# RWKV recurrence with row-packed operands and 64-row products on one Trainium2 core

## The chip, the cores and the metric

The kernel runs on 1 core of one Trainium2 chip. The metric is the device time of one execution in microseconds. Before the change the median of 3 runs is 1753.23 us (1751.1 to 1754.99).

## What is computed

A decoder trunk of two layers on 512 positions of width 1024, all in float32. Each layer has a token mixer of three branches (RWKV-7 time mixing, chunked retention, a spatial gating unit), gates that merge them, and a gated MLP with a short convolution. The change touches the RWKV-7 branch alone, whose core is a recurrence over positions, for 8 heads with a state of 64 x 64 each:

```python
S_t = S_{t-1} (diag(w_t) - kk_t^T (a_t * kk_t)) + v_t^T k_t
y_t = S_t r_t
```

Here w is a decay per channel, k, v and r are projections of the input, and kk is the normalised key.

## The kernel before, in words

**Layout.** Activations lie transposed: 128 channels on the partitions, 512 positions along the free dimension. A tile of 128 channels holds two heads, head h = 0 on partitions 0 to 63 and h = 1 on 64 to 127. Four such tiles, m = 0 to 3, hold the 8 heads. The list `hv` holds the two partition halves.

**Projections.** All large products are split in three: a float32 operand becomes a high part (a rounded copy made by ScalarE, L134) and a low part (the remainder, made by VectorE, L135), and three matmuls (L151) sum high x low, high x high and low x high. A weight unit is 128 x 512 and feeds 12 matmuls of 128 x 512. Units are loaded by DMA, split a few units ahead, and used in a fixed order.

**The recurrence in chunks.** The 512 positions are cut into 8 chunks of 64. Within a chunk the recurrence becomes products of 64 x 64 matrices and one triangular solve.

`prep(m)` (L459 to L527), once for each m, makes the chunk operands on VectorE, ScalarE and GpSimd:
- decayed copies of r and kk (the tile `ag`, L494 and L496) and of kk * a and k (`bk`, L500 and L504). They are written per head, on 64 partitions at a time, because `ag` keeps the two heads in separate free positions: `ag[hv[h], h]` holds the operands of head h, and `ag[hv[1-h], h]` later holds the products of the same head, so that one 128-row operand carries the state's part and v's part together;
- their products for every chunk (L511, 64 rows to 128 columns), which ScalarE copies from PSUM into `GB` and into `ag` (L514, L515), and GpSimd masks to be causal (L505);
- a scaling of `bk` by the decay ratio `F` between chunks, on GpSimd (L520);
- a row sum by the matrix `bonesR` (L524, L525), and VectorE's product with v (L526).

The calls of `prep` alternate with the projections of the next tile (L532 to L543).

`solve` (L667 to L727) inverts the triangular matrices on VectorE, in blocks of 32, with small matmuls for the off-diagonal block (L714, L723).

The chunk loop (L572 to L646) then runs chunk after chunk. `W[c]` is a tile of 128 rows per head: the state on one half of the partitions and v on the other (`vpair`, L558 to L566, brings v there by a transpose). For each chunk:
1. TensorE transposes `bk` (L582); ScalarE copies the result to `bt` (L586).
2. With 128 rows at once, `ag` times `w` gives the part of y (L592) and of x (L595) that come from the state and v.
3. x is copied to `xb`, half by ScalarE, half by VectorE (L596, L597).
4. 64-row products: `bt` times v into the next state `pn` (L603), and the solved `GB` times `xb` into `pu` (L605).
5. `pu` is copied over the state's half of `w` (L606, L607).
6. 64-row products of that with `bt` into `pn` (L612) and with `GB` into y (L614).
7. VectorE adds the scaled old state `fS` to `pn`, per head (L622), which writes the state half of the next `W`. GpSimd scales it for the chunk after (L626).

**What sets the order.** Between steps 2, 4 and 6 stand fills: `self.fill(n, True)` issues the next pieces of other work, mainly the gate projections (12 matmuls each), so that TensorE has something to do while a result is copied. The matmuls of the chunk loop are kept in program order by `po`; other instructions are put in order by a scheduler when the kernel is built. PSUM holds 4 tiles `sm` for this work and 4 tiles `acc` for the large products. A `fill(35)` stands inside `solve`.

Of the kernel before, what the change touches and what calls it, by code (L numbers as in the profile page):

```python
# [17 lines left out]
S = 512  # L18
# [5 lines left out]
FILL = (35, 2, 1)  # L24
# [23 lines left out]
class Emit:  # L48
# [345 lines left out]
    def rwkv(self, l, nst):  # L394
        nc, V, A, a = self.nc, self.nc.vector, self.nc.scalar, self.a
        T, P = nc.tensor, nc.gpsimd
        q8 = lambda t: t.rearrange("p (c t) -> p c t", t=64)
        pcol = lambda n, w: self.pc[:, PC[n]:PC[n] + w]
        omu = self.small((128, 14), "omu", bufs=1)
        po = self.tc.keep_in_program_order if l == 0 else lambda i: i  # L400
# [7 lines left out]
        nkk = self.small((128, 4), "nkk")  # L408
# [41 lines left out]
        hv = [slice(0, 64), slice(64, 128)]  # L450
        AG, BK, Vf, bv = [], [], [], []
        kc, rc = [], []

        def cols3(m):
# [4 lines left out]
        def prep(m):  # L459
# [8 lines left out]
            ag = self.rw((128, 2, 8, 128), "ag", 4)  # L468
# [16 lines left out]
            Eout = ci  # L485
# [4 lines left out]
            V.reciprocal(f, cx[:, 1:8, 0])  # L490
            V.tensor_tensor(f, f, cx[:, 0:7, 64], op=MUL)
            A.activation(tha, pA, AF.Tanh, scale=0.5, bias=haw[:, m:m + 1])
            for h in range(2):
                V.tensor_tensor(ag[hv[h], h, :, 64:128], q8(r)[hv[h]], Ein[hv[h]], op=MUL)  # L494
            for h in range(2):
                V.scalar_tensor_tensor(ag[hv[h], h, :, 0:64], q8(k)[hv[h]], self.p("kk", m)[hv[h]], Eex[hv[h]], op0=MUL, op1=MUL)  # L496
            V.scalar_tensor_tensor(kkn, tha, 1.0, k, op0=ADD, op1=MUL)
            A.activation(tha, tha, AF.Identity, scale=hka[:, m:m + 1], bias=oka[:, m:m + 1])
            for h in range(2):
                V.scalar_tensor_tensor(bk[hv[h], :, h, :], q8(kkn)[hv[h]], nkk[hv[h], m:m + 1], q8(Eout)[hv[h]], op0=MUL, op1=MUL)  # L500
            kp = k
            V.tensor_tensor(kp, k, tha, op=MUL)
            for h in range(2):
                V.tensor_tensor(bk[hv[h], :, 1 - h, :], q8(kp)[hv[h]], q8(Eout)[hv[h]], op=MUL)  # L504
            causal = lambda t: P.affine_select(t, t, [[0, 8], [1, 2], [1, 64]], ALU.is_ge, 0.0, base=-1, channel_multiplier=-1)  # L505
            for g in range(2):
                pgs = [self.sm((128, 4, 128)) for _ in range(2)]
                for j in range(4):
                    c = 4 * g + j
                    for h in range(2):  # L510
                        T.matmul(pgs[h][:, j, :], bk[hv[h], c, :, :].rearrange("p a t -> p (a t)"), ag[hv[h], h, c, :], start=True, stop=True)  # L511
                for h in range(2):
                    o = 1 - h
                    A.copy(GB[hv[h], 8 * m + 4 * g:8 * m + 4 * g + 4, :], pgs[h][hv[h]])  # L514
# [12 lines left out]
            AG.append(ag); BK.append(bk); bv.append(kp)  # L527

        if l == 0:
            V.memset(self.rst[:, 0:512:64], 0.0)  # L530
# [20 lines left out]
        self.solve(GB, n2)  # L551


        W, yT = [None] * 8, []
        fS = None
        po = self.tc.keep_in_program_order

        def vpair(c):  # L558
            pv = self.sm((128, 4, 128))
            for m in range(4):  # L560
                po(T.transpose(pv[:, m, :], Vf[m][:, c * 64:c * 64 + 128], self.c("ident")))
            wp = self.rw((128, 2, 4, 2, 64), "cs", 3)
            for i in range(2):
                W[c + i] = wp[:, i]
                for h in range(2):
                    A.copy(W[c + i][hv[1 - h], :, h, :], pv[hv[i], :, 64 * h:64 * h + 64])  # L566

        self.fill(1, True)
        vpair(0)
        for h in range(2):  # L570
            P.memset(W[0][hv[h], :, h, :], 0.0)
        for c in range(8):  # L572
            if c % 2 == 0:
                y = self.r(n="y")
            self.fill(FILL[2], True)
            if c % 2 and c < 7:
                vpair(c + 1)
            w = W[c]
            if c < 7:
                pb = self.sm((128, 4, 128))  # L580
                for m in range(4):
                    po(T.transpose(pb[:, m, :], BK[m][:, c, :, :].rearrange("p a t -> p (a t)"), self.c("ident")))  # L582
                if c % 2 == 0:
                    bts = self.rw((128, 2, 4, 128), "cs", 3)
                bt = bts[:, c % 2]
                A.copy(bt, pb)  # L586

            pxy = self.sm((128, 2, 4, 64))
            px, py = pxy[:, 0], pxy[:, 1]
            for m in range(4):  # L590
                for h in range(2):
                    po(T.matmul(py[hv[1 - h], m, :], AG[m][:, h, c, 64:128], w[:, m, h, :], start=m == 0, stop=False, skip_group_check=True))  # L592
            for m in range(4):
                for h in range(2):
                    po(T.matmul(px[hv[h], m, :], AG[m][:, h, c, 0:64], w[:, m, h, :], start=False, stop=True, skip_group_check=True))  # L595
            A.copy(xb[hv[0]], px[hv[0]])  # L596
            V.tensor_copy(xb[hv[1]], px[hv[1]])  # L597
            self.fill(FILL[2] + (c == 0), True)
            pu, pn = self.sm((128, 4, 64)), self.sm((128, 4, 64))
            for m in range(4):  # L600
                if c < 7:
                    for h in range(2):
                        po(T.matmul(pn[hv[h], m, :], bt[hv[1 - h], m, hv[h]], w[hv[1 - h], m, h, :], start=m == 0, stop=False, skip_group_check=True))  # L603
                for h in (1, 0):
                    po(T.matmul(pu[hv[h], m, :], GB[hv[h], 8 * m + c, 0:64], xb[hv[h], m, :], start=m == 0, stop=True, skip_group_check=True))  # L605
            A.copy(w[hv[0], :, 0, :], pu[hv[0]])  # L606
            V.tensor_copy(w[hv[1], :, 1, :], pu[hv[1]])  # L607
            self.fill(FILL[2], True)
            for m in range(4):
                if c < 7:  # L610
                    for h in range(2):
                        po(T.matmul(pn[hv[h], m, :], bt[hv[h], m, hv[h]], w[hv[h], m, h, :], start=False, stop=True, skip_group_check=True))  # L612
                for h in (1, 0):
                    po(T.matmul(py[hv[1 - h], m, :], GB[hv[h], 8 * m + c, 64:128], w[hv[h], m, h, :], start=False, stop=True, skip_group_check=True))  # L614
            if c < 7:
                wn = W[c + 1]
                for h in range(2):
                    d = wn[hv[h], :, h, :]
                    if c == 0:
                        V.tensor_copy(d, pn[hv[h]])  # L620
                    else:
                        V.tensor_tensor(d, pn[hv[h]], fS[hv[h]], op=ADD)  # L622
# [44 lines left out]
    def solve(self, G, n2):  # L667
# [18 lines left out]
        TS = self.rw((128, 32, 32), "cs", 3)  # L686
        TMP = self.rwp.tile([128, 288], F32, name=self.nm("TMP"))
# [506 lines left out]
```

## Time and profile before

| | |
|---|---|
| median of 3 runs | 1753.23 us (1751.1 to 1754.99) |
| the profiled execution | 1751.58 us |
| its span, first to last instruction | 1749.8 us |
| mean granted TensorE clock | 0.998 |
| TensorE busy in the span | 99% |
| VectorE, ScalarE, GpSimd busy | 66%, 45%, 11% |

The profile is of one execution. A group row gives the line, the engine, the operation, the tiles (out, then in), the shape and the count; then the busy time in us and the mean duration in ns; then the idle time of the engine just before these instructions, with what ended it. A timeline row gives the start in us from the start of the span, the duration in us, the engine and the instruction, with a count where equal neighbours are merged; a bracket gives the idle time before it. PE is TensorE, DVE VectorE, ACT ScalarE, POOL GpSimd. A float32 matmul of the small products appears as two records.

### The profile page before, as it was taken

What the parts mean: (1) busy time and instruction counts of PE and PEld (TensorE: products, weight loads), DVE (VectorE), ACT (ScalarE), POOL (GpSimd) and SP (SyncE); (2) the same over time, 40 slices, a digit from 0 to 9 for tenths busy, and PEclk for the clock granted to TensorE, in tenths of its full rate; (3) what the DMA queues carried; (4) which work ended last, traced back from release to release, by engine and by line L of the source; (5) the groups of instructions that cost most, each with busy time, mean ns of one, the idle gap of its engine ahead of it and who ended that gap; (6) DMA issues with size and microseconds to landing.
All of it is one profiled execution on the core that took longest, in us unless ns stands there. A gap on an engine that the chain in (4) does not pass through costs nothing.

```text
span 1749.8 us, 26360 instructions
## 1 busy us (share of the span) xinstructions
PE 1730.2 (99%) x9910; PEld 1428.4 (82%) x9910; DVE 1161.9 (66%) x1968; ACT 787.1 (45%) x1343; POOL 184.0 (11%) x195
## 2 busy tenths in 40 slices
PE   9999999999999999999999999999999999999997
PEld 7877877888888888888888788778888888888887
DVE  6888845568658777753368876455685687777433
ACT  6564444534345444333355544445343454443322
POOL 1132011003200000000013110110132000000000
PEclk9999999999999999999999999999999999999999
DMA  5224432424442332243331343234254422222332
GB/s 177 85 91 136 136 101 94 132 68 163 163 139 98 99 97 98 67 121 117 109 114 61 98 144 127 92 99 137 67 181 144 138 98 97 97 97 67 103 99 82
DMA packets 104542, 193.83 MB, mean 111 GB/s; under 512 B 12128, under 2 KB 16480, under 8 KB 104416
## 3 DMA queue, kind: packets, MB, share of 16 engines
q1 hardware_dynamic: 89568, 159.69, 28.2%
q10 hardware_dynamic: 10368, 17.78, 3.1%
q0 software_dynamic: 4480, 14.68, 2.6%
q8 instruction: 78, 1.28, 0.3%
q14 instruction: 48, 0.39, 0.1%
HBM read 175.33 MB, written 16.78 MB: 110 GB/s over the span
## 4 chain that ended last, share of the span: by engine, by line
PE 88%; DVE 5%; issue 3%; ACT 2%; DMA 1%; POOL 0%; ACTq 0%; POOLq 0%; DVEq 0%
PE acc L151 82%; PE sm L811 1%; DVE wl L135 1%; DVE ag L496 1%; DVE bk L500 1%; PE sm L592 1%; ACT ag L515 0%; DVE cs L482 0%; ACT GB L514 0%; PE sm L916 0%; PE sm L595 0%; PE sm L612 0%; PE sm L603 0%; PE sm L511 0%; DVE ag L494 0%
## 5 line engine op out<-in xcount | busy, mean ns | idle before, releaser
L151 PE MATMUL acc<-lo,sh 128*128 128x512 f32 x1108 | 432.9, 391 | 0.0
L151 PE MATMUL acc<-hi,sh 128*128 128x512 f32 x1108 | 432.0, 390 | 0.0
L151 PE MATMUL acc<-hi,sl 128*128 128x512 f32 x1108 | 430.9, 390 | 0.0
L134 ACT CAST sh<-wr 128x512 fp32r<-128x512 f32 (+1 forms) x389 | 235.9, 611 | 388.9 <-PE acc L151 300.6
L135 DVE TENSOR_TENSOR sl<-wr,sh 128x512 fp32r<-128x512 f32 (+1 forms) x389 | 262.6, 679 | 185.5 <-PE acc L151 88.8
L151 PEld LDWEIGHTS acc<-lo,sh 128*128 128x128 f32 x1108 | 208.1, 188 | 43.9 <-issue 0.7
L151 PEld LDWEIGHTS acc<-hi,sl 128*128 128x128 f32 x1108 | 208.1, 188 | 43.2
L151 PEld LDWEIGHTS acc<-hi,sh 128*128 128x128 f32 x1108 | 208.1, 188 | 42.7
L151 PE MATMUL acc<-hi,wl 128*128 128x512 f32 x588 | 229.7, 392 | 6.4 <-DVE wl L135 6.4
L151 PE MATMUL acc<-lo,wh 128*128 128x512 f32 x588 | 233.0, 396 | 1.3 <-DVE lo L210 1.3
L151 PE MATMUL acc<-hi,wh 128*128 128x512 f32 x588 | 229.5, 390 | 0.0
L151 PE MATMUL acc<-ah,sh 128*128 128x512 f32 (+1 forms) x748 | 219.4, 377 | 0.0
L135 DVE TENSOR_TENSOR wl<-wr,wh 128x512 fp32r<-128x512 f32 x195 | 142.0, 729 | 115.9 <-ACT wh L134 114.9
L134 ACT CAST wh<-wr 128x512 fp32r<-128x512 f32 x195 | 120.2, 618 | 202.6 <-PE acc L151 172.9
L151 PEld LDWEIGHTS acc<-ah,sh 128*128 128x128 f32 x748 | 137.7, 188 | 25.6
L151 PE MATMUL acc<-ah,sl 128*128 128x512 f32 (+1 forms) x374 | 140.9, 377 | 0.0
L151 PEld LDWEIGHTS acc<-hi,wl 128*128 128x128 f32 x588 | 110.4, 188 | 31.5 <-DVE wl L135 8.4
L151 PEld LDWEIGHTS acc<-lo,wh 128*128 128x128 f32 x588 | 110.4, 188 | 25.5 <-ACT wh L134 1.5
L151 PEld LDWEIGHTS acc<-hi,wh 128*128 128x128 f32 x588 | 110.5, 188 | 21.9
L967 DVE TENSOR_TENSOR fu<-acc,rsF 128x512 f32<-128x512 f32 x88 | 60.8, 690 | 69.5 <-PE acc L151 69.4
L969 ACT ACTIVATE cv<-fu,pc 128x512 f32<-128x512 f32 x88 | 71.9, 817 | 44.0 <-DVE fu L967 39.4
L151 PEld LDWEIGHTS acc<-ah,sl 128*128 128x128 f32 x374 | 70.4, 188 | 12.9
(289 smaller groups left out, 2150.7 us busy)
## 6 DMA issues: line engine op xcount, KB each, us to landing
wr<-wall SPq DMA_DIRECT2D x488, 256.0 KB, 2.6
wr<-wdn SPq DMA_DIRECT2D x80, 256.0 KB, 2.6
gd<-gth ACTq DMA_DIRECT2D x48, 256.0 KB, 3.2
gth<-gd POOLq DMA_DIRECT2D x48, 256.0 KB, 3.4
tab<-rot ACTq DMA_DIRECT2D x8, 256.0 KB, 3.6
xi<-xT SPq DMA_DIRECT2D x8, 256.0 KB, 3.4
wr<-wdn SPq DMA_DIRECT2D x16, 128.0 KB, 2.1
xd<-xi POOLq DMA_DIRECT2D x8, 256.0 KB, 2.6
```

The source lines that it names most:

```text
L134: self.kept(self.nc.scalar.copy(hi[:, :n], raw[:, :n]))
L135: self.kept(self.nc.vector.tensor_tensor(lo[:, :n], raw[:, :n], hi[:, :n], op=SUB))
L151: i = self.nc.tensor.matmul(*x, **y)
L496: V.scalar_tensor_tensor(ag[hv[h], h, :, 0:64], q8(k)[hv[h]], self.p("kk", m)[hv[h]], Eex[hv[h]], op0=MUL, op1=MUL)
L500: V.scalar_tensor_tensor(bk[hv[h], :, h, :], q8(kkn)[hv[h]], nkk[hv[h], m:m + 1], q8(Eout)[hv[h]], op0=MUL, op1=MUL)
L592: po(T.matmul(py[hv[1 - h], m, :], AG[m][:, h, c, 64:128], w[:, m, h, :], start=m == 0, stop=False, skip_group_check=True))
L811: po(T.matmul(X[h][:, i, :], lhsT, rhs, start=new[h], stop=stop, skip_group_check=True))
L967: V.tensor_tensor(u, ps, self.rsF, op=MUL)
L969: A.activation(t, u, AF.Identity, scale=self.p("cw2", j), bias=self.p("cb", j))
```

## The change

The operands of both heads are packed by rows: tile `X` holds r's and kk's decayed copies, head 0 on partitions 0 to 63 and head 1 on 64 to 127, so that each is written by one operation on 128 partitions; tile `Y` holds the products with k, in the same way, with the heads' halves exchanged. `bk` is written in two operations in place of four.

With the state `St` and v (`Vt`) in separate tiles, each 128-row product of the chunk loop becomes two 64-row products: `X` with the state (in the stretch at the start of the chunk), and `Y` with v (moved into the stretch with `bt` and `xb`; for x, a chunk ahead, into the next chunk's tile `Q`). The products in `prep` are cut in two as well, by columns.

The decay ratio `F` no longer scales `bk` on GpSimd. VectorE adds the update to the state and multiplies the sum by `F`, on 128 partitions. The copies to `xb` and `U` are one operation each (VectorE, ScalarE); `bt` is copied in three pieces. The mask on `GB` covers its right half alone; `solve` zeroes one block of it by memset.

```diff
-        xb = self.rwp.tile([128, 4, 64], F32, name=self.nm("XB"))
+        xb, U, St = [self.rwp.tile([128, 4, 64], F32, name=self.nm(n)) for n in ("XB", "U", "S")]
...
-            for h in range(2):
-                V.tensor_tensor(ag[hv[h], h, :, 64:128], q8(r)[hv[h]], Ein[hv[h]], op=MUL)
-            for h in range(2):
-                V.scalar_tensor_tensor(ag[hv[h], h, :, 0:64], q8(k)[hv[h]], self.p("kk", m)[hv[h]], Eex[hv[h]], op0=MUL, op1=MUL)
+            V.tensor_tensor(x[:, :, 64:128], q8(r), Ein, op=MUL)
+            V.scalar_tensor_tensor(x[:, :, 0:64], q8(k), self.p("kk", m), Eex, op0=MUL, op1=MUL)
...
-            for h in range(2):
-                V.scalar_tensor_tensor(bk[hv[h], :, h, :], q8(kkn)[hv[h]], nkk[hv[h], m:m + 1], q8(Eout)[hv[h]], op0=MUL, op1=MUL)
+            V.scalar_tensor_tensor(bk[:, :, 0, :], q8(kkn), nkk[:, m:m + 1], q8(Eout), op0=MUL, op1=MUL)
...
-            for h in range(2):
-                V.tensor_tensor(bk[hv[h], :, 1 - h, :], q8(kp)[hv[h]], q8(Eout)[hv[h]], op=MUL)
+            V.tensor_tensor(bk[:, :, 1, :], q8(kp), q8(Eout), op=MUL)
...
-                    for h in range(2):
-                        T.matmul(pgs[h][:, j, :], bk[hv[h], c, :, :].rearrange("p a t -> p (a t)"), ag[hv[h], h, c, :], start=True, stop=True)
-                for h in range(2):
-                    o = 1 - h
-                    A.copy(GB[hv[h], 8 * m + 4 * g:8 * m + 4 * g + 4, :], pgs[h][hv[h]])
-                    A.copy(ag[hv[o], h, 4 * g:4 * g + 4, :], pgs[h][hv[o]])
+                    for h in range(2):
+                        i = T.matmul(pK[hv[1 - h], j, :], bk[hv[h], c, 1, :], x[hv[h], c, :], start=True, stop=True)
+                        if c or h:
+                            po(i)
+                        po(T.matmul(pB[hv[h], j, :], bk[hv[h], c, 0, :], x[hv[h], c, :], start=True, stop=True))
+                A.copy(GB[:, 8 * m + 4 * g:8 * m + 4 * g + 4, :], pB)
+                A.copy(y[:, 4 * g:4 * g + 4, :], pK)
             for h in range(2):
-                causal(GB[hv[h], 8 * m:8 * m + 8, :].rearrange("p c (a t) -> p c a t", a=2))
-                causal(ag[hv[1 - h], h].rearrange("p c (a t) -> p c a t", a=2))
-            d = bk[:, 0:7].rearrange("p c a t -> p c (a t)")
-            P.tensor_tensor(d, d, f.unsqueeze(2).to_broadcast([128, 7, 128]), op=MUL)
+                yr, gr = y[hv[h]].rearrange("p c (a t) -> p c a t", a=2), GB[hv[h], 8 * m:8 * m + 8, 64:128]
+                P.affine_select(yr, yr, [[0, 8], [1, 2], [1, 64]], ALU.is_ge, 0.0, base=-1, channel_multiplier=-1)
+                P.affine_select(gr, gr, [[0, 8], [1, 64]], ALU.is_ge, 0.0, base=0, channel_multiplier=-1)
...
+        self.fill(FILL[2], True)
+        Q = self.sm((128, 2, 4, 64))
+        for m, h in mh:
+            mm(Q[hv[h], 1, m, :], Y[m][hv[1 - h], 0, 0:64], Vt[0][hv[1 - h], m, :], m == 0)
         for c in range(8):
...
-            for m in range(4):
-                for h in range(2):
-                    po(T.matmul(py[hv[1 - h], m, :], AG[m][:, h, c, 64:128], w[:, m, h, :], start=m == 0, stop=False, skip_group_check=True))
-            for m in range(4):
-                for h in range(2):
-                    po(T.matmul(px[hv[h], m, :], AG[m][:, h, c, 0:64], w[:, m, h, :], start=False, stop=True, skip_group_check=True))
-            A.copy(xb[hv[0]], px[hv[0]])
-            V.tensor_copy(xb[hv[1]], px[hv[1]])
-            self.fill(FILL[2] + (c == 0), True)
+            if c % 2 == 0 and c < 6:
+                vpair(c + 2)
+            for m, h in mh if c else ():
+                mm(P1[hv[1 - h], 0, m, :], X[m][hv[h], c, 64:128], St[hv[h], m, :], m == 0)
+                mm(Q[hv[h], 1, m, :], X[m][hv[h], c, 0:64], St[hv[h], m, :])
+            V.tensor_copy(xb, Q[:, 1])
+            if c < 7:
+                A.copy(bt[:, :, 0:64], pb[:, :, 0:64])
+                for h in range(2):
+                    A.copy(bt[hv[h], :, 64:128], pb[hv[1 - h], :, 64:128])
+            self.fill(FILL[2], True)
+            Q = self.sm((128, 2, 4, 64)) if c < 7 else None
+            for i in (0, 4, 5, 6, 7, 1, 2, 3):
+                for h in range(2):
+                    m, o = i % 4, 1 - h
+                    if c < 7 and i < 4:
+                        mm(Q[hv[h], 0, m, :], bt[hv[o], m, hv[h]], Vt[c][hv[o], m, :], m == 0)
+                    elif c < 7:
+                        mm(Q[hv[h], 1, m, :], Y[m][hv[o], c + 1, 0:64], Vt[c + 1][hv[o], m, :])
+                    if i < 4:
+                        mm(P1[hv[h], 1, m, :], GB[hv[h], 8 * m + c, 0:64], xb[hv[h], m, :], c == m == 0)
+                    else:
+                        mm(P1[hv[o], 0, m, :], Y[m][hv[o], c, 64:128], Vt[c][hv[o], m, :])
+            A.copy(U, P1[:, 1])
+            self.fill(FILL[2], True)
+            for m, h in mh:
+                mm(P1[hv[1 - h], 0, m, :], GB[hv[h], 8 * m + c, 64:128], U[hv[h], m, :])
                 if c < 7:
+                    mm(Q[hv[h], 0, m, :], bt[hv[h], m, hv[h]], U[hv[h], m, :])
             if c < 7:
-                wn = W[c + 1]
-                for h in range(2):
-                    d = wn[hv[h], :, h, :]
-                    if c == 0:
-                        V.tensor_copy(d, pn[hv[h]])
-                    else:
-                        V.tensor_tensor(d, pn[hv[h]], fS[hv[h]], op=ADD)
-                if c < 6:
-                    fS = self.rw((128, 4, 64), "fS", 2)
-                    for h in range(2):
-                        P.tensor_tensor(fS[hv[h]], wn[hv[h], :, h, :], F[hv[h], :, c + 1:c + 2].to_broadcast([64, 4, 64]), op=MUL)
+                f = F[:, :, c:c + 1].to_broadcast([128, 4, 64])
+                if c == 0:
+                    V.tensor_tensor(St, Q[:, 0], f, op=MUL)
+                else:
+                    V.tensor_tensor(St, St, Q[:, 0], op=ADD)
+                    V.tensor_tensor(St, St, f, op=MUL)
...
+        for h in range(2):
+            self.nc.gpsimd.memset(G[64 * h + 32:64 * h + 64, :, 0:32], 0.0)
```

More of the change, by code (lines that the diff above doesn't have):

```diff
@@ L467, in prep @@
                 T.matmul(o, w[:, ms], xh, start=False, stop=True)
-            ag = self.rw((128, 2, 8, 128), "ag", 4)
+            x, y = [self.rw((128, 8, 128), n, 4) for n in ("X", "Y")]
             bk = self.rw((128, 8, 2, 64), "bk", 4)
@@ L526, in prep @@
             V.tensor_tensor(kp, v, pbn, op=MUL)
-            AG.append(ag); BK.append(bk); bv.append(kp)
+            X.append(x); Y.append(y); BK.append(bk); bv.append(kp)
         if l == 0:
@@ L551, in rwkv, with mm @@
         self.solve(GB, n2)
-        W, yT = [None] * 8, []
-        fS = None
-        po = self.tc.keep_in_program_order
+        Vt, yT, mh = [None] * 8, [], [(m, h) for m in range(4) for h in range(2)]
+        def mm(o, l, r, start=False):
+            po(T.matmul(o, l, r, start=start, stop=True, skip_group_check=True))
         def vpair(c):
@@ L574, in rwkv @@
                 y = self.r(n="y")
[L575 to L578, printed above, removed]
+            if c:
+                self.fill(FILL[2], True)
+            P1 = self.sm((128, 2, 4, 64))
             if c < 7:
@@ L594, in rwkv @@
                 for h in range(2):
-                    po(T.matmul(px[hv[h], m, :], AG[m][:, h, c, 0:64], w[:, m, h, :], start=False, stop=True, skip_group_check=True))
-            A.copy(xb[hv[0]], px[hv[0]])
-            V.tensor_copy(xb[hv[1]], px[hv[1]])
-            self.fill(FILL[2] + (c == 0), True)
-            pu, pn = self.sm((128, 4, 64)), self.sm((128, 4, 64))
-            for m in range(4):
-                if c < 7:
-                    for h in range(2):
-                        po(T.matmul(pn[hv[h], m, :], bt[hv[1 - h], m, hv[h]], w[hv[1 - h], m, h, :], start=m == 0, stop=False, skip_group_check=True))
-                for h in (1, 0):
-                    po(T.matmul(pu[hv[h], m, :], GB[hv[h], 8 * m + c, 0:64], xb[hv[h], m, :], start=m == 0, stop=True, skip_group_check=True))
@@ L606, in rwkv @@
[L606 to L610, printed above, removed]
-                    for h in range(2):
-                        po(T.matmul(pn[hv[h], m, :], bt[hv[h], m, hv[h]], w[hv[h], m, h, :], start=False, stop=True, skip_group_check=True))
-                for h in (1, 0):
-                    po(T.matmul(py[hv[1 - h], m, :], GB[hv[h], 8 * m + c, 64:128], w[hv[h], m, h, :], start=False, stop=True, skip_group_check=True))
@@ new lines, in rwkv @@
+            A.copy(U, P1[:, 1])
+            self.fill(FILL[2], True)
+            for m, h in mh:
+                mm(P1[hv[1 - h], 0, m, :], GB[hv[h], 8 * m + c, 64:128], U[hv[h], m, :])
+                if c < 7:
+                    mm(Q[hv[h], 0, m, :], bt[hv[h], m, hv[h]], U[hv[h], m, :])
+            if c < 7:
+                f = F[:, :, c:c + 1].to_broadcast([128, 4, 64])
[4 more added lines that the diff above has]
+                    V.tensor_tensor(St, St, f, op=MUL)
@@ L627, in rwkv @@
+            py = P1[:, 0]
             yr = hv[c % 2]
```

17 lines of the change are left out of this document (6 added, 11 removed).

## The prediction

> **What bounds the kernel now.** I read the page first: engine shares, then the chain that ended last by engine.
>
> ```profile
> span 1749.8 us, 26360 instructions
> PE 1730.2 (99%) x9910; PEld 1428.4 (82%) x9910; DVE 1161.9 (66%) x1968; ACT 787.1 (45%) x1343; POOL 184.0 (11%) x195
> ...
> PE 88%; DVE 5%; issue 3%; ACT 2%; DMA 1%; POOL 0%; ACTq 0%; POOLq 0%; DVEq 0%
> ```
>
> TensorE is busy all the way; VectorE, the next, has a third of the span free. So the question is what the change does to the stream of matmuls, and to the few places where that stream stops. The waits of PE name them, and PE's own timeline shows the four of the first group (each pair: the last matmul before the stop and the first after it).
>
> ```profile
> PE acc L151 <- DVE wl L135: 6.4, 4, 2.7
> ```
>
> ```profile
> 106.62 0.39 PE L151 MATMUL acc<-lo,wh 128*128 128x512 f32 x1
> 106.84 0.39 PE L151 MATMUL acc<-hi,wh 128*128 128x512 f32 x1
> 108.58 0.50 PE L151 MATMUL acc<-hi,wl 128*128 128x512 f32 x1 [1.35 <-DVE wl L135]
> ...
> 132.50 0.39 PE L151 MATMUL acc<-hi,wh 128*128 128x512 f32 x1
> 134.89 0.50 PE L151 MATMUL acc<-hi,wl 128*128 128x512 f32 x1 [2.00 <-DVE wl L135]
> ...
> 969.21 0.39 PE L151 MATMUL acc<-hi,wh 128*128 128x512 f32 x1
> 970.02 0.51 PE L151 MATMUL acc<-hi,wl 128*128 128x512 f32 x1 [0.42 <-DVE wl L135]
> ...
> 993.06 0.39 PE L151 MATMUL acc<-hi,wh 128*128 128x512 f32 x1
> 996.11 0.50 PE L151 MATMUL acc<-hi,wl 128*128 128x512 f32 x1 [2.66 <-DVE wl L135]
> ```
>
> Matmuls follow each other every 0.22 to 0.23 us (first two rows). Start to start the four stops take 1.74, 2.39, 0.81 and 3.05 us; less 0.23 each, the stream loses 1.51 + 2.16 + 0.58 + 2.82 = **7.07 us**. (The brackets give less, because a matmul's modelled end lies behind the next start.) All four are in `prep`, two per layer, and all wait for the low half of a weight, which VectorE splits off at L135 between `prep`'s own operations.
>
> **The change part by part.**
>
> *VectorE in prep.* Here is its queue ahead of the second stop, and the late split of the other three.
>
> ```profile
> 127.16 0.68 DVE L135 TENSOR_TENSOR wl<-wr,wh 128x512 fp32r<-128x512 f32 x1
> ...
> 129.49 1.51 DVE L500 SCALAR_TENSOR_TENSOR bk<-cs,nkk,cs 64x512 f32<-64x512 f32 x2
> ...
> 131.15 1.33 DVE L494 TENSOR_TENSOR ag<-rwc,cs 64x512 f32<-64x512 f32 x2
> 132.50 1.51 DVE L496 SCALAR_TENSOR_TENSOR ag<-rwc,pc,cs 64x512 f32<-64x512 f32 x2
> ...
> 134.18 0.65 DVE L135 TENSOR_TENSOR wl<-wr,wh 128x512 fp32r<-128x512 f32 x1
> ```
>
> ```profile
> 107.84 0.69 DVE L135 TENSOR_TENSOR wl<-wr,wh 128x512 fp32r<-128x512 f32 x1
> ...
> 969.27 0.69 DVE L135 TENSOR_TENSOR wl<-wr,wh 128x512 fp32r<-128x512 f32 x1
> ...
> 995.36 0.69 DVE L135 TENSOR_TENSOR wl<-wr,wh 128x512 fp32r<-128x512 f32 x1
> ```
>
> Each split ends just before its matmul starts. Between two splits stand six half operations, 64 partitions each. The change makes them three of 128 partitions. Does a full one cost what a half one does?
>
> ```profile
> L496 DVE SCALAR_TENSOR_TENSOR ag<-rwc,pc,cs 64x512 f32<-64x512 f32 x16 | 12.0, 748 | 0.2
> L500 DVE SCALAR_TENSOR_TENSOR bk<-cs,nkk,cs 64x512 f32<-64x512 f32 x16 | 12.0, 747 | 1.6 <-ACT cs L486 1.3
> L504 DVE TENSOR_TENSOR bk<-rwc,cs 64x512 f32<-64x512 f32 x16 | 11.0, 686 | 0.4
> L494 DVE TENSOR_TENSOR ag<-rwc,cs 64x512 f32<-64x512 f32 x16 | 10.6, 663 | 0.1
> L502 DVE TENSOR_TENSOR rwc<-rwc,cs 128x512 f32<-128x512 f32 x8 | 5.5, 686 | 0.0
> ```
>
> It does: L504 on 64 partitions and L502 on 128 both take 686 ns. So half of 12.0 + 12.0 + 11.0 + 10.6 = 45.6 us goes: 22.8 us of VectorE, 2.85 us per `prep`. That isn't itself time of the kernel; it counts only where the stream waits. Ahead of a late split, one each of L500, L494 and L496 goes: 0.75 + 0.66 + 0.75 = 2.16 us. The four stops are 1.51, 2.16, 0.58 and 2.82 us, so with nothing else moved min(2.16, stop) goes from each: 1.51 + 2.16 + 0.58 + 2.16 = 6.41 us. The remaining 0.66 us should go too: earlier `prep`s free VectorE in the same way (so the queue ahead of the fourth stop begins earlier), and in the changed kernel's listed order fewer operations stand between two splits there. I take all 7.07 us; bounds: 0 (the queue order puts a split late elsewhere) and 7.07.
>
> *The order.* I compared the listed order of both kernels' instructions, engine by engine. TensorE meets `prep`'s four blocks of products 13, 23, 37 and 66 matmuls earlier than now in the first layer (9 to 50 in the second), and the product with `bonesR` 3 matmuls behind each block instead of 12 to 16. These waits are new in place.
>
> ```profile
> 53.49 1.51 DVE L500 SCALAR_TENSOR_TENSOR bk<-cs,nkk,cs 64x512 f32<-64x512 f32 x2 [0.17 <-ACT cs L486]
> ```
>
> ```profile
> 65.30 2.06 PE L511 MATMUL sm<-ag,bk 64*128 64x128 f32 x32
> 67.29 0.50 PE L151 MATMUL acc<-hi,wh 128*128 128x512 f32 x1
> ```
>
> ```profile
> L514 ACT COPY GB<-sm 64x512 f32<-64x512 f32 x32 | 18.4, 575 | 1.9 <-PE sm L511 1.5 <-ACT gth L377 0.4
> L482 DVE TENSOR_TENSOR_SCAN cs<-rst,cs 128x512 f32<-128x512 f32 x8 | 12.7, 1593 | 3.9 <-ACT cs L481 3.8
> ```
>
> I walked VectorE's listed order with the durations above. Ahead of the first block, from 53.5 us on, stand two scalar_tensor_tensors, three tensor_tensors, three splits and two short ones before `bk` is complete, about 2 × 0.75 + 6 × 0.68 + 0.4 = 6.0 us, so 59.5 us. The block stands 13 matmuls ahead of its place at 65.30, at 65.3 − 13 × 0.227 = 62.3 us: 2.8 us to spare. The tightest place that I found is in the second layer's last `prep`: from the arrival of the decay's product, two steps of ScalarE (about 1.5 us), the scan (1.6) and twelve listed operations up to a split (about 7.5) make 10.6 us, and TensorE has 53 matmuls or their equal, 12.0 us, before it needs that split: 1.4 us to spare. If one slips, the stream waits by the slip. The product with `bonesR` reuses a PSUM tile that ScalarE has to empty with the second of two copies (0.58 us each) after half the block; those end about when the product is due, so up to 0.3 us each could be lost: 0 to 2.4 us over eight; I take 0.
>
> *ScalarE and GpSimd in prep.* Four full copies replace eight halves; the scaling by F leaves GpSimd, one of its two masks per head is half as long, two memsets per layer come. Neither engine is waited for by PE in `prep` now; what needs them first is `solve`, and its first product stands behind fill(35), 35 × 12 × 0.227 = 95 us of matmuls. I cost them at 0; without that cover it would be a few of their operations, 0.6 to 1.6 us each as above.
>
> *TensorE.* The total of its own work is the big unknown. An fp32 product leaves two records (L592: 8 products, x16).
>
> ```profile
> 263.16 0.22 PE L612 MATMUL sm<-cs,cs 64*64 64x64 f32 x2
> 263.17 0.23 PE L614 MATMUL sm<-cs,GB 64*64 64x64 f32 x2
> ...
> 263.45 0.23 PE L612 MATMUL sm<-cs,cs 64*64 64x64 f32 x2
> ...
> 267.06 0.69 PE L592 MATMUL sm<-cs,ag 128*64 128x64 f32 x16
> 267.58 0.64 PE L595 MATMUL sm<-cs,ag 128*64 128x64 f32 x16
> ```
>
> L612 and L614 are 64-row products into all four quadrants (two row halves, two column halves). Four records start within 0.01 us, and the row at 263.45 begins the fifth round after 263.16: 0.058 us a round, so four products (two rounds) take 0.117 us. The 128-row products of L592 take 0.52 us for eight: two column halves run at a time. Now count a chunk c = 1 to 6. Before: 16 products of 128 rows, 2 × 0.52 = 1.04 us, plus 16 + 16 of 64 rows, 8 × 0.117 = 0.94. After: 16 + 32 + 16 products of 64 rows, all ordered so that four in a row meet four quadrants: 16 × 0.117 = 1.87 us. So 1.98 against 1.87. Chunks 0 and 7 come out alike: products that use two quadrants only are as many before as after. The number of stretches between fills stays, and so do the changes of array shape. In `prep`, 16 products of 64×128 become 32 of 64×64, four at a time instead of two: the 1.99 us of the block (65.30 to 67.29) stay. Bounds: −0.11 × 14 chunks = −1.5 us, and, if only two quadrants ever ran together, +1.87 × 14 + 1.99 × 8 = +42 us. I take 0, nearest to the rows at 263.
>
> *Hand-overs in the recurrence.* The state's scaling moves from GpSimd (off the path) to VectorE (on it).
>
> ```profile
> L566 ACT COPY cs<-sm 64x256 f32<-64x256 f32 x32 | 11.7, 366 | 0.6
> L622 DVE TENSOR_TENSOR cs<-sm,fS 64x256 f32<-64x256 f32 x24 | 10.1, 421 | 0.7
> L597 DVE COPY XB<-sm 64x256 f32<-64x256 f32 x16 | 6.8, 427 | 13.3 <-ACT XB L596 13.1
> ```
>
> Before, two half adds (0.84 us) make the next state; after, one full add and one full multiply, about the same. The cover is the fill, 12 matmuls × 0.227 = 2.7 us, and each hand-over (`xb`, `U`, the state) is one or two operations of about 0.4 us behind at most one 0.7 us filler operation: 1.6 us. The tightest place is ScalarE in chunks 0, 2 and 4: four copies of `vpair` and three of `bt`, 7 × 0.37 = 2.6 us against some 2.7 to 3.5. If it slips, what waits is the stretch with `xb`; 0 to 0.5 us each, six times: 0 to 3 us. I take 0.
>
> **Sum.** The profiled execution took 1751.58 us (span 1749.8): 1751.6 − 7.1 = 1744.5. It lies 1.65 us below the median of its three runs, 1753.23; against that median the forecast is **1746 us**.
>
> **Rivals.**
>
> *The stops move.* Splits or products late in new places eat the gain: the `bonesR` product (2.4), `vpair` in chunks 0, 2, 4 (3), one of the four stops left (0.6 to 2.8). Speaks for it: the block of products now stands earlier. Against: every place that I walked has slack. Half of it eaten gives 1750, all of it 1753.
>
> *Quadrants don't run four at a time* (the slower side). Place: all 64-row products. Price: 42 us if two at a time, 1753 − 7 + 42 = 1788. It decides from 7.07 / 42 = 17% of the overlap lost. For it: the new stretches are up to 32 products long, and neighbours in them share rows. Against: in L612 and L614 neighbours share rows too (h = 1 of both), and those four start together. [...]
>
> *More than the stops goes.* If the 1.5 us of the recurrence comes too: 1744.
>
> *The change does nothing:* if the splits are late for their casts or DMAs instead of VectorE, 1753; the rows above show the VectorE queue full up to each split, so little.
>
> **How the numbers follow.** Stops go, stream unchanged (1743 to 1749): 0.75. Stops move and eat most: 0.14, around 1751. Quadrants lose overlap, in part or whole: 0.08, from 1755 up. More goes: 0.03. The range 1742 to 1752 holds the first and the fourth and most of the second. About 0.2%, 3.5 us, is what a measurement of this kernel can tell from no change: faster 0.79, same 0.12, slower 0.09.
>
> **What would show it.** Right: PE's waits for L135 in `prep` vanish, VectorE's sum falls by about 20 us, stretches of 64-row products keep 0.058 us a round, and the time falls by no more than about 8 us. Wrong: a new row of PE waiting for ScalarE or VectorE in the recurrence or at the `bonesR` product; rounds of 0.117 us; or `prep`'s block of 2 us growing to 4.

## The result and the profile after

The changed kernel takes **1743.79 us** (median of 6 runs, 1743.3 to 1746.81) against 1755.28 us for the kernel before (6 runs beside it, 1751.1 to 1757.29). The ratio is 0.9941, with a 95% interval of 0.9928 to 0.9955: 7.9 to 12.6 us less, 10.4 in the middle. The profiled execution took 1744.99 us. These lines of its page are the span, the busy times, and the shares of the chain that ended last.

```profile
span 1743.3 us, 27599 instructions
...
PE 1729.9 (99%) x10614; PEld 1427.2 (82%) x10614; DVE 1116.4 (64%) x1918; ACT 776.2 (45%) x1323; POOL 147.4 (8%) x163
...
PE 94%; issue 2%; DVE 1%; DMA 1%; ACT 1%; POOL 0%; POOLq 0%; SPq 0%; DVEq 0%; ACTq 0%
```

TensorE's busy time is what it was (1730.2 before); the chain's share on VectorE fell from 5% to 1%, and VectorE's busy time fell by 45.5 us, twice what the packed operations save. The waits of PE (us in total, times, longest):

```profile
PE acc L274 <- DVE rst L271: 1.5, 1, 1.5
PE acc L151 <- DVE lo L210: 1.1, 1, 1.1
PE sm L519 <- ACT Y L511: 1.0, 1, 1.0
```

No wait for L135's low half is left. One is new: L519, the product by `bonesR`, waits once for ScalarE. Start to start, from PE's own timeline:

```profile
946.39 0.40 PE L151 MATMUL acc<-hi,wh 128*128 128x512 f32 x1
947.80 0.50 PE L519 MATMUL sm<-lo,bonesR 128*128 128x512 f32 x1 [1.01 <-ACT Y L511]
```

The stream loses 1.41 − 0.23 = 1.18 us there. So the profile shows 7.07 us of stops gone and 1.18 come, a net 5.9 us; the spans differ by 6.5.

Two more differences stand in the two traces. The kernel before loses time once more, inside a block of `prep`'s products (L511), where the list of waits doesn't show it. From its first product to the matmul behind it this block takes 2.95 us, the seven others 1.99; its products start singly, not in pairs, up to 950.5 us, and the second half operation of L504, whose result they need, ends at 950.18 us (that they wait for it is inferred from these times):

```profile
949.32 3.03 PE L511 MATMUL sm<-ag,bk 64*128 64x128 f32 x32
952.27 0.50 PE L151 MATMUL acc<-hi,sh 128*128 128x512 f32 x1
```

```profile
949.49 0.69 DVE L504 TENSOR_TENSOR bk<-rwc,cs 64x512 f32<-64x512 f32 x1
```

In the changed kernel each of the eight blocks takes 1.91 us: 1.6 us less in sum. Against that, the profile after has a slower start: from 7.8 to 10.8 us TensorE runs 9 matmuls in place of 13, and its 40th record starts 1.6 us later. So without the start the spans differ by 8.1 us, of which 5.9 + 1.6 = 7.5 are accounted for. The ratio says 10.4. The rest had to be found.

VectorE's groups in `prep` (mean ns of one in the second figure behind the bar):

```profile
L497 DVE SCALAR_TENSOR_TENSOR bk<-cs,nkk,cs 128x512 f32<-128x512 f32 x8 | 6.0, 748 | 1.8 <-ACT cs L486 1.8
L494 DVE SCALAR_TENSOR_TENSOR X<-rwc,pc,cs 128x512 f32<-128x512 f32 x8 | 6.0, 746 | 0.0
...
L500 DVE TENSOR_TENSOR bk<-rwc,cs 128x512 f32<-128x512 f32 x8 | 5.5, 687 | 0.1
...
L493 DVE TENSOR_TENSOR X<-rwc,cs 128x512 f32<-128x512 f32 x8 | 5.2, 645 | 0.0
```

A full operation costs what a half one did: 22.7 us in place of 45.6. And two groups that nobody touched became shorter; first before, then after:

```profile
L429 DVE SCALAR_TENSOR_TENSOR rwc<-rwp,pc,rwc 128x511 f32<-128x511 f32 x28 | 26.5, 957 | 5.6 <-ACT rwc L428 5.5
```

```profile
L429 DVE SCALAR_TENSOR_TENSOR rwc<-rwp,pc,rwc 128x511 f32<-128x511 f32 x28 | 22.0, 796 | 4.6 <-ACT rwc L428 4.3
...
L482 DVE TENSOR_TENSOR_SCAN cs<-rst,cs 128x512 f32<-128x512 f32 x8 | 10.3, 1285 | 1.4 <-ACT cs L481 1.3
```

L429 fell by 4.5 us, the scan L482 by 2.4 (1593 ns each before). The traces tie this to what GpSimd does beside them: before, 13 of the 28 L429 run beside a GpSimd instruction and take 1203 ns on average, the other 15 take 743; after, it is 4 at 1090 ns and 24 at 747.

### The profile page after: what moved, and what is told of

Its sections match the earlier page's. It is cut to its first block, busy times and chain, and to the rows that moved or that the text cites. A ratio compares the mean times of both kernels' runs of the same rounds, so it can differ in the third digit from the quotient of the medians.

```text
span 1743.3 us, 27599 instructions
## 1 busy us (share of the span) xinstructions
PE 1729.9 (99%) x10614; PEld 1427.2 (82%) x10614; DVE 1116.4 (64%) x1918; ACT 776.2 (45%) x1323; POOL 147.4 (8%) x163
## 4 chain that ended last, share of the span: by engine, by line
PE 94%; issue 2%; DVE 1%; DMA 1%; ACT 1%; POOL 0%; POOLq 0%; SPq 0%; DVEq 0%; ACTq 0%
PE acc L151 87%; PE sm L554 2%; PE sm L808 1%; PE sm L506 1%; DMA wr<-wall 0%; PE sm L913 0%; PE sm L581 0%; PE sm L151 0%; PE sm L478 0%; PE acc L274 0%; DMA ws<-sgw 0%; DMA tab<-rot 0%; PE sm L836 0%; PE sm L863 0%; PE sm L787 0%
## 5 line engine op out<-in xcount | busy, mean ns | idle before, releaser
L135 DVE TENSOR_TENSOR sl<-wr,sh 128x512 fp32r<-128x512 f32 (+1 forms) x389 | 261.9, 677 | 191.3 <-PE acc L151 90.0
L135 DVE TENSOR_TENSOR wl<-wr,wh 128x512 fp32r<-128x512 f32 x195 | 139.7, 718 | 141.0 <-ACT wh L134 139.6
```

What stands on the lines that cost most here:

```text
L135: self.kept(self.nc.vector.tensor_tensor(lo[:, :n], raw[:, :n], hi[:, :n], op=SUB))
```

## The experiments

The theory: VectorE's queue in `prep` makes TensorE's stops, and the packing shortens that queue. The rivals: the gain lies in the recurrence, in GpSimd's lighter load, or in something that the profile of one execution doesn't show. Each ratio is against the kernel before, run beside it.

**VectorE's load alone put back.** In the changed kernel:

```diff
-            V.tensor_tensor(x[:, :, 64:128], q8(r), Ein, op=MUL)
+            for s in hv:
+                V.tensor_tensor(x[s, :, 64:128], q8(r)[s], Ein[s], op=MUL)
...
-            V.tensor_tensor(bk[:, :, 1, :], q8(kp), q8(Eout), op=MUL)
+            for s in hv:
+                V.tensor_tensor(bk[s, :, 1, :], q8(kp)[s], q8(Eout)[s], op=MUL)
```

> The changed kernel with the four packed VectorE operations of prep (X's two, bk's two) each cut into two of 64 partitions, so that VectorE gets back 16 x (0.75 + 0.75 + 0.69 + 0.66) / 2 = 22.8 us and nothing else changes. Theory (VectorE's queue ahead of the weight splits made the stops): stops waiting for L135's low half come back in prep, up to the 7.07 us of before, fewer if what GpSimd left counts too; 1747 to 1751. Rival (the gain comes from the recurrence, from GpSimd or from the end of the layers): no such stop, 1744, within 1.5 us of the changed kernel.

Measured: 1752.27 us (12 runs, 1751.28 to 1754.99), ratio 0.9983 (0.9975 to 0.9992). So 1752.27 − 1743.79 = 8.5 us are gone again with these eight half operations for each `prep` (7.4 by the ratios), a little more than the theory had said. The place is another. PE's waits in this kernel:

```profile
PE sm L523 <- ACT Y L515: 4.9, 3, 2.1
...
PE acc L151 <- DVE wl L135: 1.1, 2, 0.8
```

Most of the stops came back at the `bonesR` product (here L523), not at the splits. The largest of them, by PE's and then ScalarE's timeline:

```profile
88.16 0.40 PE L151 MATMUL acc<-lo,wh 128*128 128x512 f32 x1
90.64 0.50 PE L523 MATMUL sm<-lo,bonesR 128*128 128x512 f32 x1 [2.09 <-ACT Y L515]
```

```profile
88.20 0.72 ACT L428 ACTIVATE rwc<-rwp,omu 128x512 f32<-128x512 f32 x1 [0.84 <-DVE rwp L426]
89.40 0.72 ACT L428 ACTIVATE rwc<-rwp,omu 128x512 f32<-128x512 f32 x1 [0.48 <-DVE rwp L426]
90.03 0.57 ACT L515 COPY Y<-sm 128x512 f32<-128x512 f32 x1
90.49 0.59 ACT L514 COPY GB<-sm 128x512 f32<-128x512 f32 x1
```

Read it from below. The product needs a PSUM tile that the copies empty; the copies stand in ScalarE's queue behind two L428 of the next projections; these wait for VectorE (L426). A late VectorE thus reaches TensorE by way of ScalarE too. In the changed kernel the one stop that is left (at 947.80) has the same two L428 ahead of it:

```profile
945.94 1.34 ACT L428 ACTIVATE rwc<-rwp,omu 128x512 f32<-128x512 f32 x2 [0.84 <-DVE rwp L426]
947.18 0.56 ACT L511 COPY Y<-sm 128x512 f32<-128x512 f32 x1
```

**GpSimd's load alone put back.** In the changed kernel, `ones1` being a tile of ones:

```diff
+            d = bk[:, 0:7].rearrange("p c a t -> p c (a t)")
+            P.tensor_tensor(d, d, self.ones1.unsqueeze(2).to_broadcast([128, 7, 128]), op=MUL)
```

> The changed kernel with the multiply of bk put back on GpSimd, by a tile of ones (the decay stays on VectorE, so the values stay as they are): 8 x 1.8 = 14.4 us of GpSimd come back. Theory (no instruction of TensorE waits for GpSimd in prep): 1744, within 1.5 us. Rival (GpSimd's work lengthens VectorE's beside it: L429 took 957 ns in before and 796 ns in the changed kernel, the scan L482 1593 and 1285, and their sums fell by 6.9 us): part of the gain goes, 1746 to 1748, and L429's or L482's mean rises.

Measured: 1744.97 us (6 runs), ratio 0.9943 (0.9929 to 0.9957); L429 took 804 ns. No loss that can be told: the multiply on GpSimd is not what the gain is made of.

**Both together.** The two diffs above in one kernel.

> Both edits together: VectorE's four operations of prep in halves, and the multiply of bk on GpSimd by ones. Prep's load is then nearly that of before, and the recurrence is that of the changed kernel. Theory (all of the gain lies in prep's load on VectorE): 1750 to 1755, four stops of about 7 us in sum. Rival (a part of the gain lies in the recurrence): stops as before and yet 3 us or more below the kernel before.

Measured: 1754.54 us (12 runs), ratio 0.9995 (0.9986 to 1.0003): all of the gain is gone, though the recurrence is the new one. The recurrence is therefore neutral, within about 2.5 us; in the traces its stretches of small products, each from the first product to the matmul behind it, sum to 48.2 us in the second profile of before (shown below) and to 48.3 in the changed kernel. Against the first experiment, whose 12 runs were taken beside these, the median is 2.3 us higher: 9 of the 12 runs here lie above 1753.4 us, and 2 of the 12 there. So once VectorE is full GpSimd's multiply costs some 2 us, and the trace shows a way: L429 takes 975 ns on average in place of 851, and the stops at the `bonesR` product, which stand where they stood there, are longer (6.3 us in place of 4.9):

```profile
PE sm L527 <- ACT Y L517: 6.3, 3, 3.2
```

**The kernel before, weights split earlier.**

```diff
-AHEAD = {None: 2, "p": 4, "r": 3, "f": 3, "u": 5}
+AHEAD = {None: 2, "p": 6, "r": 3, "f": 3, "u": 5}
```

> The kernel before, with the weight units of prep split up to 6 ahead in place of 4, nothing packed. Theory (a split is late because it stands behind prep's operations in VectorE's queue, and the stop is all that it costs): most of the four stops go without any packing, so 1748 to 1750, 5 to 7 us below the kernel before. Rival (VectorE hasn't the time in prep at all, or buffers come free no sooner): the stops stay or move, within 2 us of the kernel before.

Measured: 1756.1 us (12 runs), ratio 1.0003 (0.9994 to 1.0011), and PE's wait as it was:

```profile
PE acc L151 <- DVE wl L135: 6.8, 4, 3.0
```

The rival holds. A setting that lets the splits go further ahead gives VectorE no time to do so. Whether it is the time or the buffers that bind wasn't told apart.

**VectorE relieved in the kernel before, by GpSimd.**

```diff
-                V.tensor_tensor(ag[hv[h], h, :, 64:128], q8(r)[hv[h]], Ein[hv[h]], op=MUL)
+                P.tensor_tensor(ag[hv[h], h, :, 64:128], q8(r)[hv[h]], Ein[hv[h]], op=MUL)
```

> The kernel before with r's decayed copy (L494, two operations of 0.66 us for each prep) on GpSimd in place of VectorE, nothing packed: 10.6 us leave VectorE. Theory (VectorE's queue makes the stops): about 1.33 us of each stop go, 1.33 + 1.33 + 0.58 + 1.33 = 4.6 us, so 1750 to 1752, if bk's products don't wait for the slower GpSimd. Rival (GpSimd's operations lengthen VectorE's beside them, or the stops hang on something else): within 2 us of the kernel before, and L429 or the scan longer than 957 and 1593 ns.

Measured: 1765.32 us (6 runs), ratio 1.0063 (1.0049 to 1.0077): slower by 11 us by the ratio and by 8.8 by the medians, a miss beyond both numbers. Three groups say why; the first two cost 748 and 747 ns in the kernel before.

```profile
L496 DVE SCALAR_TENSOR_TENSOR ag<-rwc,pc,cs 64x512 f32<-64x512 f32 x16 | 18.7, 1168 | 0.1
...
L500 DVE SCALAR_TENSOR_TENSOR bk<-cs,nkk,cs 64x512 f32<-64x512 f32 x16 | 16.7, 1044 | 1.9 <-ACT cs L486 1.7
```

```profile
L494 POOL TENSOR_TENSOR ag<-rwc,cs 64x512 f32<-64x512 f32 x16 | 22.1, 1384 | 63.2 <-ACT cs L487 62.6
```

10.6 us left VectorE, and L496 and L500 grew by 6.7 + 4.7 = 11.4 us beside the GpSimd operation, which itself takes twice as long (1384 ns against 663). The relief was nil, and `bk` and the copies came later: TensorE's stops for L135 stayed, and two rows of waits came.

```profile
PE acc L151 <- DVE wl L135: 6.8, 3, 2.7
PE sm L511 <- DVE bk L504: 4.1, 2, 2.6
PE sm L524 <- ACT ag L515: 3.7, 2, 2.0
```

The rival's mechanism held, with other lines than it had named: L429 and the scan did not grow (927 and 1426 ns here, 957 and 1593 in the kernel before), L496 and L500 did.

**The kernel before, profiled again.**

> The kernel before once more, for a second profile: the profiled execution of before lay 3.6 us below the median of its runs (1751.58 against 1755.14 of 29). Theory (prep's stops are most of what differs from execution to execution, since a late queue adds up): a span above 1749.8 us comes with more than 7.07 us of stops. Rival (the spread has another place): the four stops stay at 7.1 us within 0.3, whatever the span.

Measured: 1756.4 us, span 1754.6 us, clock 0.996. The four stops are 1.56 + 2.18 + 0.58 + 2.82 = 7.14 us: as before, while the span is 4.8 us longer. The rival holds: the stops' length is not what varies. What varies stands behind them. PE's timeline at the second stop in this profile, and then at the same place in the first:

```profile
134.70 0.39 PE L151 MATMUL acc<-hi,wh 128*128 128x512 f32 x1
137.11 0.59 PE L151 MATMUL acc<-hi,wl 128*128 128x512 f32 x1 [2.02 <-DVE wl L135]
137.50 0.63 PE L151 MATMUL acc<-lo,wh 128*128 128x512 f32 x1
137.92 0.63 PE L151 MATMUL acc<-hi,wh 128*128 128x512 f32 x1
```

```profile
135.22 0.40 PE L151 MATMUL acc<-lo,wh 128*128 128x512 f32 x1
135.46 0.39 PE L151 MATMUL acc<-hi,wh 128*128 128x512 f32 x1
```

Behind the stop the matmuls come every 0.39 to 0.42 us in place of 0.23. The view by windows gives the mean granted clock of each stretch (the number ahead of the last two):

```profile
134.00:137.00 3.00, 1.08 (x5) 0.56 (x3) 2.93 (x7) 0.61 (x1) 0.00 (x0) 1.00 0.00 0
137.00:140.60 3.60, 3.49 (x9) 2.73 (x10) 3.57 (x8) 0.63 (x1) 0.00 (x0) 0.55 0.54 123
...
1000.60:1004.20 3.60, 3.55 (x9) 2.81 (x10) 3.57 (x7) 0.63 (x1) 0.00 (x0) 0.55 0.48 150
```

The clock falls to 0.55, as a mean over 3.6 us, behind the second stop (2.41 us start to start) and behind the fourth (3.05), 9 matmuls each, some 9 x 0.19 = 1.7 us lost each time (an estimate from the rows above). In the first profile stops of 2.39 and 3.05 us cost nothing more; the clock behind them is 1.00. The rest of the 4.8 us is put down to the slower start (107 matmuls in the first 30 us in place of 116), which the changed kernel's profile has as well (109).

The mean clocks go with it: 0.998 in the first profile and 0.996 in the second, and two stretches of 3.6 us at 0.55 take off 2 x 3.6 x 0.45 / 1754.6 = 0.0018. The profiled executions of the four experiments above with long stops have 0.997 (VectorE's load alone), 0.996 (both together), 0.998 (weights split earlier) and 0.996 (VectorE relieved by GpSimd); where in them the clock fell was not shown.

So a long stop may cost its length and, in a part of the executions, some 1.7 us on top: the author's estimate, from the second profile. If so, filling the stops should make the kernel before faster.

**The stops filled with useless work.** In the kernel before, `zero` being a tile of zeros and `extra` 8 and 11 at the two matmuls that wait longest:

```diff
+        for _ in range(extra):
+            mm(ps, self.zero, xh, start=False, stop=False)
         mm(ps, wl, xh, start=False, stop=stop)
```

> The kernel before with 8 and 11 matmuls more (by a tile of zeros, so that the sums stay as they are) right ahead of the two matmuls that wait longest for L135, at 134.89 and 996.11 us: 19 x 0.2275 = 4.3 us of added work in stops of 2.39 and 3.05 us (start to start), which it fills. In the second profile of before the granted clock fell to 0.55 for 3.6 us behind just these two stops, which cost 1.7 us each; in the first it did not. Theory (an idle TensorE of 2 to 3 us lets the clock fall behind it in a part of the executions, and that is what the stops cost beyond their length): with the stops filled the median falls by 2 to 3 us, to 1752 to 1754, though work was added, and most runs show 0.997 to 0.998 in place of 0.996. Rival (the spread has another cause): no change, within 1 us of before; or slower by what doesn't fit into the stops.

Measured: 1753.2 us (11 runs, 1752.1 to 1754.75), ratio 0.9988 (0.9980 to 0.9997), 2.35 us less by the medians (0.5 to 3.5 by the interval) with 4.3 us of work added. Of the 11 runs 9 show a mean clock of 0.998 and 2 of 0.997; of 55 runs of the kernel before only 4 show 0.998, 16 show 0.997 and 35 show 0.996 (medians 1751.7, 1754.2 and 1756.2 us). The fourth stop is filled, and the clock holds behind it (in the rows below 0.34 us from start to start, then every 0.23 us):

```profile
995.54 2.65 PE L154 MATMUL acc<-hi,zero 128*128 128x512 f32 x11
998.36 0.50 PE L154 MATMUL acc<-hi,wl 128*128 128x512 f32 x1 [0.17 <-DVE wl L137]
998.70 0.39 PE L154 MATMUL acc<-lo,wh 128*128 128x512 f32 x1
```

**The changed kernel, profiled again.**

> The changed kernel once more, for a second profile and for more runs with their granted clocks. Theory (without long stops in prep the clock holds): nearly all runs at 0.997 to 0.998, and no stretch of half clock in prep but for the start; 1743 to 1745. Rival: runs at 0.996 as often as before.

Measured: 1744.62 us (5 runs, 1743.88 to 1745.42), ratio 0.9938 (0.9926 to 0.9951), 4 runs at 0.998 and one at 0.997; the profiled execution has a mean of 0.998. In the first profile of this kernel the clock is 1.00 in the `prep`s of both layers (30 to 140 and 860 to 1010 us). The theory holds. (One stop is new in this profile: 0.6 us for an L135, at 320 us, behind the first layer's recurrence.)

**The order of the quadrants.** In the changed kernel each stretch of the recurrence is ordered by row half (the last stretch is shown; the other two alike):

```diff
+        hm = [(m, h) for h in range(2) for m in range(4)]
...
-            for m, h in mh:
+            for m, h in hm:
                 mm(P1[hv[1 - h], 0, m, :], GB[hv[h], 8 * m + c, 64:128], U[hv[h], m, :])
```

> The changed kernel with each stretch of 64-row products in the recurrence ordered by row half (all products that read partitions 0 to 63 first), so that neighbours meet two quadrants in place of four; the products themselves are the same. Theory (four quadrants run together when four in a row meet them, two when only two are met): each product then takes 0.058 us in place of 0.029, 64 products a chunk, 1.87 us more for each of 14 chunks: 26 us, 1766 to 1774. [...]

Measured: 1766.54 us (4 runs, 1764.37 to 1767.2), ratio 1.0057 (1.0043 to 1.0072): about 20 us more than the changed kernel by the ratios, where 26 were expected. The stretch of 16 products and the one of 32, each from its first product to the matmul behind it, in the changed kernel and then here:

```profile
262.37 0.69 PE L554 MATMUL sm<-S,X 64*64 64x64 f32 x32
262.99 0.50 PE L151 MATMUL acc<-wl,hi 128*128 128x512 f32 x1
...
265.93 0.27 PE L554 MATMUL sm<-cs,cs 64*64 64x64 f32 x1
...
267.02 0.50 PE L151 MATMUL acc<-wl,hi 128*128 128x512 f32 x1
```

```profile
254.95 0.97 PE L555 MATMUL sm<-S,X 64*64 64x64 f32 x32
255.85 0.50 PE L151 MATMUL acc<-wl,hi 128*128 128x512 f32 x1
...
258.84 0.27 PE L555 MATMUL sm<-cs,cs 64*64 64x64 f32 x1
...
260.68 0.50 PE L151 MATMUL acc<-wl,hi 128*128 128x512 f32 x1
```

0.62 becomes 0.90, and 1.09 becomes 1.84: the same products, with neighbours that meet two quadrants in place of four. Four quadrants do run together in the changed kernel, with both row halves writing into one PSUM tile: within its stretch of 32, four records, one of each quadrant, start from 266.74 to 266.76 us.

**The `bonesR` product later.** In the changed kernel it is issued behind the next tile's projections:

```diff
-            pbn = self.sm()
-            T.matmul(pbn, self.bonesR, kl, start=True, stop=False)
-            T.matmul(pbn, self.bonesR, kh, start=False, stop=True)
-            V.tensor_tensor(kp, v, pbn, op=MUL)
+            late.append((kp, kh, kl, v))
```

> The changed kernel with the product by bonesR issued after the next tile's projections, so that it stands 12 to 14 matmuls behind its block in place of 3 in the first two preps of the first layer and about alike in the second. Theory (the one stop of 1.18 us that is left in prep waits for a PSUM tile that ScalarE empties late): that stop goes and nothing else comes, about 1 us less by the trace, 1743; whether it shows in the median is doubtful. Rival (what takes the tile next waits in its place): a stop of about 1 us at another product, 1744.

Measured: 1744.37 us (5 runs), ratio 0.9934 (0.9922 to 0.9946), a profiled span of 1741.5 us but no median that can be told from the changed kernel's. The stop at `bonesR` went, and a smaller one came at another product (L477), so each side is half right. The L135 in the second row is not new: it stands at 318 us, behind the recurrence, where the changed kernel's second profile waits too.

```profile
PE sm L477 <- ACT Y L522: 0.6, 1, 0.6
PE acc L151 <- DVE wl L135: 0.4, 1, 0.4
```

**The state's multiply on GpSimd.** In the changed kernel:

```diff
-                    V.tensor_tensor(St, St, f, op=MUL)
+                    P.tensor_tensor(St, St, f, op=MUL)
```

> The changed kernel with the state's multiply by F (one operation of 128x256 a chunk, from chunk 1 on) on GpSimd in place of VectorE. GpSimd took 624 ns for 64x256 in before, so the hand-over of the state grows by some 0.5 us, behind a fill of 2.7 us. Theory (each hand-over of the recurrence has more than 0.5 us of slack): 1744, within 1.5 us of the changed kernel, and no wait of TensorE for the state. Rival (the multiply on the path is what the recurrence waits for): up to 0.5 us for each of 12 chunks, 1750.

Measured: 1745.87 us (4 runs), ratio 0.9946 (0.9931 to 0.9961), no wait of PE for the state in its profile. The median is 1.25 us above that of the changed kernel's 5 runs beside it, within what was expected: no loss that can be told. The hand-over has room.

## Why the prediction was right, point by point

- **The stops go (7.07 us).** Right: all four are gone. With VectorE's four operations in halves again 8.5 us come back, so the load on VectorE is the cause. But then TensorE stops at the `bonesR` product (4.9 us) and hardly at L135 (1.1): in the new order a late VectorE shows at another place.
- **Which wait would be left.** The `bonesR` product was put at 0, bounded by 0.3 us each. It costs 1.18 us once; a new row of waits there stood among the prediction's own signs of being wrong. The place and the cause (a PSUM tile that ScalarE empties late) were right; the bound for one was too small, since only the copies' own time was counted and not what stands ahead of them in ScalarE's queue, two L428 that wait for VectorE. With VectorE full it is the main stop.
- **VectorE's sum falls by about 20 us.** It fell by 45.5: 22.9 by the packed operations, 6.9 by L429 and the scan, the rest in smaller groups. It is busy time, not the kernel's.
- **TensorE's own work unchanged, rounds of 0.058 us.** Right for the recurrence: a chunk's stretch of 32 products takes 1.09 us, and all stretches together take 48.2 us before and 48.3 after. `prep`'s blocks were put at an unchanged 1.99 us; they take 1.91, and one of them held a wait of 0.96 us before that the prediction did not see: together 1.6 us put at nothing. The rival (quadrants not together) was priced at 42 us with 26 of it in the recurrence; with pairs forced it cost 20 there. It was right to go by the rows at 263 us, where four records start within 0.01 us: in the changed kernel's stretch of 32 four start within 0.02.
- **Hand-overs at 0.** Right, also with the multiply on GpSimd.
- **GpSimd's part at 0.** Right for the changed kernel (1744.97 with its multiply put back), not with VectorE full (some 2 us). That VectorE's operations are longer beside GpSimd's (L429: 1203 ns in place of 743) was not considered.
- **The sum.** 7.1 us were forecast and 10.4 measured (7.9 to 12.6), where the prediction had named a fall of no more than about 8 us as its sign. The main term that failed is the price of a stop: it was its length alone. The two profiles of before and the filled stops show the other part, some 1.7 us of low clock behind each of the stops of 2.41 and 3.05 us, in one of the two profiles. The profile used for the working lay at 0.998, where few runs of that kernel lie. At a clock of 0.998 the kernels differ by some 7 to 8 us (1751.7 against 1743.7 and 1744.7 in its two sets of runs), and the traces account for 7.5; the remaining 2 to 3 us fit the clock, of which filling two stops gave back 2.35.
- **The time itself.** The forecast of 1746 us lies 2.2 us from the 1743.79 measured, nearer than the fall does (3.3 us by the ratio, 4.4 by the medians). That is luck: the base, a median of three runs at 1753.23 us, was 2 us lower than that of the 55 later runs, 1755.38, and this made up for part of the fall that was missing.

What stays open: why a stop of 3.05 us is followed by a low clock in one execution and not in another; and whether the time or the buffers keep the splits from going further ahead.

## What to carry to other kernels

A stop of the busiest engine can be worth more than its length, as it was here where a clock of 0.55 followed for 3.6 us (some 1.7 us more): look at the granted clock behind each stop, in more than one profile, before pricing it. Here an operation on half of the partitions cost VectorE as much as one on all (748 ns each), so packing two halves halved what they cost; moving 10.6 us of VectorE's work to GpSimd instead cost VectorE 11.4 us in other operations. When a queue is relieved or filled again, follow it through the engine between: here VectorE held up TensorE by way of ScalarE's copies.

## What the runs showed of the hardware

- Behind stops of 2.41 and 3.05 us TensorE ran at a mean granted clock of 0.55 over 3.6 us in one execution; in another, behind stops of 2.39 and 3.05 us, it ran at 1.00.
- Two of VectorE's operations of 64x512 (L496, L500) took 1168 and 1044 ns on average in place of 748 and 747 with a GpSimd operation beside them; L429 (128x511) took 1203 ns on average beside a GpSimd instruction and 743 without.
- 64-row products that meet two quadrants in turn took 1.84 us for 32, and 1.09 us when neighbours meet four, with both row halves writing into the same PSUM tile.
